# A hybrid decoder layer on one core: the steady plan of its recurrence in another order

## The chip, the cores and the metric

The kernel runs on one core of one Trainium2 chip. The metric is the time of one execution on the device, in microseconds (us). Three runs of the kernel before have a median of 2458.68 (2458.55 to 2462.13).

## The reference, cut to what matters

One layer over 2048 tokens of width 1024, batch 1. The change lies in the first sub-layer, whose input projection feeds two groups of heads: an SSD group and an RWKV7 group with a recurrence over the tokens.

```python
def _rwkv7_scan(r, w, k, v, za, zb):
    def step(S, inp):
        r_t, w_t, k_t, v_t, a_t, b_t = inp
        sa = jnp.einsum("bhij,bhj->bhi", S, a_t)
        S = S * w_t[:, :, None, :] + sa[..., None] * b_t[:, :, None, :] + v_t[..., None] * k_t[:, :, None, :]
        return S, jnp.einsum("bhij,bhj->bhi", S, r_t)
...
xn = _rms_norm(h, pre_mix_norm[l])
proj = (xn @ w_in[l]).astype(jnp.float32)
p_ssd, p_rwkv = jnp.split(proj, [SSD_COLS], axis=-1)
y_ssd = _ssd_mixer(p_ssd, ...)
y_rwkv = _rwkv7_mixer(p_rwkv, ...)
mix = jnp.concatenate([y_ssd, y_rwkv], axis=-1).astype(h.dtype) @ w_out[l]
h = h + _rms_norm(mix, post_mix_norm[l])
hn = _rms_norm(h, pre_ffn_norm[l])
u = _causal_dwconv(hn @ ffn_w_up[l], ffn_conv_w[l], ffn_conv_b[l])
gate, val = jnp.split(u, 2, axis=-1)
f = (jax.nn.silu(gate) * val) @ ffn_w_down[l]
h = h + _rms_norm(f, post_ffn_norm[l])
```

## The kernel before

The program has three stages: `phase_R` computes the input projections, the convolution of the SSD group and the RWKV7 recurrence in 16 blocks of 128 tokens (R0 to R15); `phase_S` does the SSD group, the output projection and the norms; `phase_F` the feed-forward part. The change touches only `phase_R` and its seam to `phase_S`.

The recurrence of a block is done in two chunks of 64 tokens with the usual triangular form: products of the scaled keys and receptances (gram), a triangular solve, and products with the state. A block's work is cut into some 295 small steps, each of which issues the instructions of one engine (a PE step a whole group of matmuls). A step is written `block.name.arguments/part`. What the parts are:

- `load`: /0 VectorE copies the halo of the token tile xt, /1 SP loads the rows, /2 ScalarE squares and sums them, /3 and /4 GpSimd the root (a power), /5 and /6 ScalarE scales and rounds, /7 GpSimd the low half, /8 and /9 SP transposes both halves into xt by DMA, /10 SP stores xt.
- `d.0` to `d.13`: a group of 24 matmuls each for 128 columns of the RWKV7 projection (line 737). Two neighbours (d.0 and d.1, and so on) share a PSUM bank. An even one is a TensorE step only. An odd one has /0 TensorE, /1 and /2 ScalarE (line 981), /3 and /4 VectorE (line 984), for both; after that the bank is free. d.0 and d.1 give WA and GL, d.2 to d.5 the keys tk, d.6 to d.9 tr, d.10 to d.13 the values tv.
- `conv.0` to `conv.7`: the same for the SSD columns. An odd one has /0 TensorE, /1 and /2 ScalarE, /3 to /8 the taps on VectorE (line 1030), /9 ScalarE tanh, /10 VectorE, /11 SP.
- `low.0`: /0, /1, /3, /5 ScalarE, /2, /4, /6 VectorE. `low.1`: /0 and /5 TensorE (zw, za), four ScalarE steps behind each.
- `scan` /0 GpSimd, /1 VectorE, /2 GpSimd, /3 and /4 ScalarE. `keys` /0 GpSimd, /1 ScalarE. `norm` /0 TensorE, /1 and /2 ScalarE, /3, /8, /9, /11 VectorE, the rest GpSimd. `receptance`: VectorE.
- `gram.0`, `gram.1`: /0 TensorE (line 1163), /1 and /2 VectorE masks.
- `solve`: /0 to /8 SP (the diagonal blocks out to memory and back, start values), /9 to /70 the substitution, 62 instructions on VectorE in one chain (lines 1203 and 1209, two inputs from SBUF each), /71 to /78 SP (the result out and back).
- `turn`: VectorE (line 1281), then `merge.0` and `merge.1`: /0 TensorE (lines 1297, 1301), /1 and /2 ScalarE.
- `own.c` /0 and /1 TensorE (pq, lines 1334 and 1340), /2 ScalarE; `update.c` /0 TensorE, /1 and /2 ScalarE; `state.c` /0 and /1 GpSimd, /2 TensorE (pS), /3 and /4 VectorE (S), /5 TensorE (pq), /6 and /7 ScalarE, which empty pq (line 1402).
- `values` /0 TensorE, /1 and /2 ScalarE, /3 TensorE, /4 VectorE. `transposed.c`: GpSimd for c = 0, one TensorE and one ScalarE step. `gate` /0 TensorE, /1 ScalarE.
- `finish.0`: /0 ScalarE, /1 VectorE, /2 GpSimd, /3 GpSimd (a power, line 1437), /4 GpSimd (line 1441). `finish.1`: /0 TensorE (yt), /1 to /4 ScalarE (line 1453), /5 and /6 GpSimd (lines 1463, 1464), /7 ScalarE, /8 GpSimd, /9 SP.

The order of every engine's queue is written out by hand. `HEAD` is the order of block 0 and much of block 1. `PLAN` is one round of the steady state and is walked 13 times (`it` = 2 to 14): `f` stands for block `it`, `n` for the one after it, `b` for `it` - 1 and `a` for `it` - 2, so that a round holds steps of up to four blocks, and each of a block's 295 steps comes in one of the rounds. A step that has been done already is skipped. `TAIL` creates what is left (in the order of the allocations), and `ORDER` gives the order in which that is issued. Each engine takes its steps strictly in the order of the text; waits between engines follow from the data and the buffers. PSUM is held in rings: two banks for the d and conv pairs, three for zw, za, nq, gr, bt, vt and bo, one each for pq (Q), for pu and pS (U), and for pw, po, zg, yt and one of the gr (B). The order of the text is also the order in which these rings are handed out.

```python
for it in range(2, iters - 1):
    for step in PLAN.split():
        ...
        n = it + {"n": 1, "f": 0, "b": -1, "a": -2}[who]
        if 0 <= n < iters:
            blocks[n].do(name, *(int(v) for v in a), only=int(part) if part else None)
```

## Time and profile before

| | us |
|---|---|
| median of three runs | 2458.68 |
| the profiled execution, its own time | 2461.38 |
| its span, first to last instruction | 2459.6 |
| TensorE busy | 2353.0 (96%) |
| VectorE busy | 1879.6 (76%) |
| ScalarE busy | 1200.3 (49%) |
| GpSimd busy | 1061.2 (43%) |

The profile is one execution. Its engines are PE (TensorE matmuls), PEld (weight loads), DVE (VectorE), ACT (ScalarE), POOL (GpSimd) and SP (the queue that issues DMAs). A timeline row has the start and the length in us, the engine, the line of the kernel, the operation, what it writes and reads, the shape and the number of instructions merged into the row, and in brackets the idle time of the engine just before it with the one who ended it. The steps of the recurrence fill about the first 800 us of the span, and a round of the plan is repeated there with the same pattern.

### The profile page before, as it was taken

The numbers are of one execution on the slowest core, as the hardware profiler recorded it, in microseconds if no ns is written. First come the engines' busy times: TensorE is split into PE (matmuls) and PEld (weight loads), VectorE is DVE, ScalarE is ACT, GpSimd is POOL, SyncE is SP. The second block draws the span as 40 slices with busy tenths as digits, with TensorE's granted clock in tenths as the row PEclk, the third lists the DMA queues.
The fourth block names the chain that finished last, engine by engine and source line by source line (L and its number), as shares of the span: only waits on it lengthen the run. The fifth ranks groups of instructions, "written<-read, shape, count | busy, mean of one in ns | idle before, by whom it ended". The sixth has DMA issues, their size and how long they took to land.

```text
span 2459.6 us, 53351 instructions
## 1 busy us (share of the span) xinstructions
PE 2353.0 (96%) x20986; PEld 1483.9 (60%) x20988; DVE 1879.6 (76%) x3790; ACT 1200.3 (49%) x2471; POOL 1061.2 (43%) x1134
## 2 busy tenths in 40 slices
...
DMA packets 344412, 319.11 MB, mean 130 GB/s; under 512 B 203232, under 2 KB 248672, under 8 KB 340832
## 3 DMA queue, kind: packets, MB, share of 16 engines
...
q14 instruction: 87, 0.71, 0.1%
...
## 4 chain that ended last, share of the span: by engine, by line
PE 40%; DVE 7%; issue 3%; POOL 3%; ACT 2%; DMA 2%; SPq 0%; POOLq 0%; DVEq 0%; ACTq 0%
PE u L2288 25%; PE d L2528 12%; DVE w L2141 1%; PE o L2002 1%; PE l L2653 1%; DVE C L2310 1%; DVE p L2345 1%; DVE a L2345 1%; POOL fa L2139 0%; DMA hs<-HN 0%; PE z L1787 0%; POOL m L2040 0%; DVE dw L2492 0%; DMA HN<-hT 0%; DVE b L2139 0%
## 5 line engine op out<-in xcount | busy, mean ns | idle before, releaser
L2288 PE MATMUL u<-b,w 128*128 128x512 f16 x3696 | 807.0, 380 | 16.3 <-DVE C L2310 7.9
L2288 PEld LDWEIGHTS <-w 128*128 128x128 f16 x3696 | 362.3, 98 | 456.1 <-issue 23.3
L737 PE MATMUL d<-xt,wr 128*128 128x129 f16 x5376 | 337.8, 224 | 34.4 <-DMA xt<-xh 14.6
L737 PEld LDWEIGHTS <-wr 128*128 128x128 f16 x5376 | 319.6, 100 | 42.5 <-issue 27.4
L2528 PE MATMUL d<-dw,fa 128*128 128x512 f16 x1512 | 334.6, 380 | 5.8 <-DVE acc L2541 3.7
L2528 PEld LDWEIGHTS <-fa 128*128 128x128 f16 x1596 | 156.5, 98 | 200.8 <-issue 13.6
L2310 DVE TENSOR_TENSOR C<-u,C 128x512 f32<-128x512 f32 x220 | 150.7, 686 | 157.0 <-PE u L2288 140.9
L737 PE MATMUL c<-xt,wc 128*128 128x131 f16 x3072 | 194.3, 224 | 4.9 <-ACT tv L981 2.8
L737 PEld LDWEIGHTS <-wc 128*128 128x128 f16 x3072 | 182.0, 98 | 9.3 <-issue 4.6
L2541 DVE TENSOR_TENSOR acc<-d,acc 128x512 f32<-128x512 f32 x212 | 139.5, 681 | 43.8 <-PE d L2528 39.7
L2139 POOL TENSOR_TENSOR fa<-p,fa 128x512 f16<-128x512 f32 x100 | 133.9, 1350 | 75.5 <-ACT fa L2134 75.5
L2345 DVE SCALAR_TENSOR_TENSOR p<-C,fpar,p 128x1024 f32<-128x1024 f32 x88 | 121.1, 1376 | 45.5 <-ACT p L2341 45.2
L1203 DVE TENSOR_TENSOR tmp<-atl,xl 128x60 f32<-128x60 f32 (+24 forms) x465 | 129.0, 277 | 11.7 <-DMA atl<-ATd 0.2
L2306 ACT ACTIVATE C<-u 128x512 f32<-128x512 f32 x88 | 52.2, 593 | 169.5 <-PE u L2288 134.8
L2141 DVE SCALAR_TENSOR_TENSOR w<-us,w 128x512 f16<-128x512 f32 x132 | 126.6, 969 | 9.4 <-ACT w L2134 8.7
L1030 DVE SCALAR_TENSOR_TENSOR ca<-c,cw,ca 128x128 f32<-128x128 f32 x360 | 114.4, 344 | 21.1 <-ACT ca L1020 17.2
L2345 DVE SCALAR_TENSOR_TENSOR a<-C,fpar,a 128x1024 f32<-128x1024 f32 x88 | 122.7, 1394 | 6.9 <-ACT a L2341 5.5
L2134 ACT ACTIVATE fa<-p 128x512 f16<-128x512 f32 x110 | 65.6, 622 | 114.5 <-DVE p L2358 87.4
L2134 ACT ACTIVATE w<-us 128x512 f16<-128x512 f32 x132 | 79.8, 624 | 80.2 <-PE u L2288 29.1
L1209 DVE TENSOR_TENSOR xl<-xl,tmp 128x60 f32<-128x60 f32 (+24 forms) x465 | 99.2, 213 | 13.9
L2261 POOL TENSOR_TENSOR us<-us,us 128x512 f32<-128x512 f32 x51 | 78.0, 1532 | 50.0 <-DVE w L2141 28.7
L1787 PE MATMUL z<-ws,xs 128*128 128x512 f16 x384 | 93.5, 386 | 0.1
...
## 6 DMA issues: line engine op xcount, KB each, us to landing
...
```

The source lines that it names most:

```text
L737: nc.tensor.matmul(ps, w[:, a, kt, :], xt[:, b, kt, cols], start=n == 0, stop=n == 3 * KT - 1)
L1030: V.scalar_tensor_tensor(out=acc[:, q], in0=m["rc", e][:, q, k:k + 128], scalar=cw[:, e + q, k:k + 1], in1=acc[:, q], op0=ALU.mult, op1=AL ...
L1203: chain.tensor_tensor(out=self.tmp[:, :k, :n], in0=self.atl[:, j, j + 1:32].unsqueeze(1).to_broadcast([P, k, n]), in1=self.xl[:, :k, j:j + ...
L1209: chain.tensor_tensor(out=self.xl[:, :k, j + 1:32], in0=self.xl[:, :k, j + 1:32], in1=self.tmp[:, :k, :n], op=ALU.add)
L2134: S.activation(h, src, AF.Copy, **({} if scale is None else {"scale": scale}))
L2139: {"V": V, "G": G_}[engine].tensor_tensor(out=l, in0=src, in1=h, op=ALU.subtract)
L2141: V.scalar_tensor_tensor(out=l, in0=src, scalar=scale, in1=h, op0=ALU.mult, op1=ALU.subtract)
L2288: nc.tensor.matmul(bk[at], self.w[i][:, u, k, :], self.half.b[i][:, k, v, :], start=start and n == 0, stop=n == 11, skip_group_check=True)
L2310: op("V", .61, lambda: V.tensor_tensor(out=part(j, x), in0=bk[at], in1=part(*a), op=ALU.add), (("u", 4 * s + at), (*(c0, c1)[a[0]], a[1])) ...
L2345: V.scalar_tensor_tensor(out=o[j], in0=C[j][:, 2 - d:1026 - d], scalar=cw(g, 2 - d), in1=o[j], op0=ALU.mult, op1=ALU.add)
L2528: nc.tensor.matmul(bk[s, t], pairs[m].a[i][:, u, t * P:t * P + P], pairs[m].w[n][0][:, v, :], start=new and m == 0 and u == v == 0, stop=m ...
L2541: V.tensor_tensor(out=acc[j][:, t], in0=bk[s, t], in1=acc[j][:, t], op=ALU.add)
```

## The change

`PLAN` is replaced by another order of a round of 295 steps. Some steps also change rounds: steps 27 to 34 of the solve, d.11/1, d.11/3, load/8, load/9, state.1/0, state.1/1 and gate/1 go from one round to the next one's start (from `f` to `b`, `n` to `f`, `b` to `a`), and state.1/6 from `a` to the end of `b`. In `TAIL`, R14.d.11 is put ahead of the list, and in `ORDER` the 15 steps that the 13 rounds now leave over are put in front; all else of both is as before (the lines are only wrapped anew).

```diff
@@ -294,37 +294,37 @@
 R1.conv.7/11 R1.solve/74 R1.solve/75 R1.solve/78 R1.solve/76 R2.load/10 R1.transposed.1/1 R1.solve/77
 """
 PLAN = """
-f.d.0 b.solve/35 a.state.1/6 a.state.1/7 b.solve/36 b.solve/37 a.finish.0/0 b.solve/38 f.d.1/0 b.d.13/2 b.conv.7/9
-b.d.13/1 a.finish.0/1 b.solve/39 b.solve/40 b.solve/41 b.solve/42 b.solve/43 b.solve/44 b.solve/45 b.solve/46
-a.finish.0/2 b.transposed.0/2 b.d.13/3 b.values/3 b.d.13/4 a.finish.0/3 f.d.1/1 f.d.1/2 f.d.2 b.conv.5/11 f.scan/2
-b.solve/47 a.finish.0/4 f.d.1/3 a.finish.1/0 f.low.0/0 b.values/0 b.solve/48 f.low.0/1 f.d.1/4 f.low.0/3 b.solve/49
-f.d.3/0 n.load/0 b.transposed.1/1 b.solve/50 b.solve/51 f.low.0/2 f.low.0/4 a.finish.1/1 b.solve/52 a.finish.1/4
-b.solve/53 a.finish.1/2 b.solve/54 a.state.1/3 a.finish.1/3 a.finish.1/5 b.solve/55 b.solve/56 f.low.1/0 f.d.4
-b.values/4 f.d.3/1 f.d.3/2 f.d.3/4 f.d.3/3 a.finish.1/6 a.finish.1/7 f.load/10 f.d.5/0 f.d.6 b.solve/57 b.solve/58
-f.low.1/1 f.low.1/3 a.state.1/4 f.d.5/2 b.solve/59 b.solve/60 b.solve/61 b.solve/62 b.solve/63 b.solve/64 b.solve/65
-f.low.1/5 f.d.5/1 b.values/1 f.d.5/3 f.d.5/4 f.low.1/4 f.low.1/6 f.keys/0 f.d.7/0 f.d.8 f.d.9/0 b.solve/66 f.low.1/2
-f.scan/0 b.solve/67 b.solve/68 f.low.1/9 b.values/2 f.d.7/2 b.conv.7/10 f.low.1/7 b.solve/69 b.solve/70 f.d.7/4
-f.d.7/1 f.d.7/3 f.scan/1 b.solve/73 f.keys/1 f.norm/0 f.low.1/8 f.norm/4 f.norm/5 f.norm/1 f.d.9/2 b.solve/72 f.d.9/1
-b.own.0/0 f.norm/7 b.solve/74 f.scan/3 f.norm/6 a.finish.1/8 b.solve/71 f.conv.0 f.norm/2 f.d.9/3 f.conv.1/0
-b.solve/75 f.d.9/4 f.norm/3 b.state.0/0 f.scan/4 f.norm/8 f.conv.1/1 f.conv.1/2 f.conv.1/4 b.own.0/1 f.conv.1/3
-b.own.0/2 f.conv.1/6 f.norm/10 b.solve/76 f.conv.1/5 f.conv.1/7 b.conv.7/11 f.conv.2 b.turn/0 b.solve/78 b.turn/1
-f.conv.1/8 f.norm/11 f.conv.1/9 f.conv.3/0 a.finish.1/9 b.merge.0/0 f.low.0/5 f.norm/12 b.solve/77 b.merge.0/1
-b.merge.0/2 f.conv.1/10 f.conv.4 b.merge.1/0 f.conv.3/1 f.conv.3/2 f.norm/9 f.receptance/0 n.load/1 b.merge.1/2
-f.gram.0/0 b.merge.1/1 f.gram.1/0 b.update.0/0 f.conv.3/4 f.receptance/1 b.update.0/1 b.update.0/2 f.conv.3/3
-f.conv.3/6 f.solve/8 b.low.0/6 f.conv.3/8 n.load/2 f.conv.3/5 f.gram.0/1 f.gram.0/2 f.conv.1/11 f.gram.1/2
-f.transposed.0/0 f.gram.1/1 n.load/3 f.conv.3/7 f.receptance/2 n.load/4 f.conv.5/0 b.gate/0 f.receptance/4 f.conv.3/9
-f.conv.3/10 b.state.0/2 b.state.0/1 b.state.0/5 f.conv.5/1 n.load/5 n.load/6 f.solve/1 b.state.0/4 f.solve/0
-f.conv.5/3 f.conv.5/5 n.load/7 f.conv.5/2 f.solve/2 f.receptance/3 f.conv.6 f.solve/3 f.conv.5/4 b.gate/1 f.conv.7/0
-b.state.0/3 b.state.0/6 b.state.0/7 b.own.1/0 f.conv.5/6 b.own.1/1 b.state.1/0 f.conv.3/11 f.conv.7/1 b.state.1/1
-f.transposed.0/1 f.conv.5/8 f.conv.5/7 f.conv.7/2 f.conv.5/9 f.conv.7/3 f.conv.7/5 f.conv.7/7 b.own.1/2 f.conv.7/4
-f.solve/4 f.conv.7/6 f.conv.7/8 f.solve/5 f.conv.5/10 f.solve/6 f.d.10 f.d.11/0 f.d.11/1 f.solve/7 n.load/8
-b.update.1/0 b.update.1/1 b.update.1/2 f.solve/9 f.d.11/2 f.solve/10 f.solve/11 f.solve/12 f.solve/13 f.solve/14
-f.solve/15 f.solve/16 f.solve/17 f.solve/18 f.solve/19 f.solve/20 f.solve/21 f.solve/22 f.d.11/3 f.solve/23 f.solve/24
-f.solve/25 f.solve/26 f.solve/27 f.solve/28 f.solve/29 f.solve/30 f.solve/31 f.solve/32 f.solve/33 f.solve/34 n.load/9
-f.transposed.1/0 f.d.12 f.d.11/4 b.state.1/5 b.state.1/2 f.d.13/0
+b.d.11/1 a.state.1/0 a.state.1/7 a.finish.0/0 b.d.11/3 b.solve/27 b.solve/28 b.transposed.0/2 f.load/8 a.state.1/1
+b.d.13/2 b.d.13/1 b.solve/29 a.finish.0/1 b.solve/30 b.solve/31 b.transposed.1/1 b.d.13/3 b.solve/32 b.solve/33
+b.d.13/4 a.gate/1 f.load/9 f.d.0 f.d.1/0 f.d.1/1 f.d.2 a.finish.0/2 a.finish.0/3 b.solve/34 b.solve/35 b.conv.5/11
+b.values/0 b.solve/36 b.solve/37 f.d.1/3 f.d.1/2 f.d.1/4 b.solve/38 b.solve/39 f.d.4 f.low.0/0 f.low.0/1 f.low.0/3
+f.low.0/2 f.low.1/0 b.conv.7/9 a.finish.0/4 a.finish.1/0 a.finish.1/1 b.solve/40 b.solve/41 b.solve/42 b.solve/43
+b.solve/44 b.solve/45 b.solve/46 b.solve/47 a.finish.1/4 b.solve/48 f.d.3/0 f.low.0/4 b.solve/49 b.solve/50 b.solve/51
+b.values/1 a.finish.1/3 a.finish.1/2 b.values/2 f.low.1/1 b.solve/52 b.solve/53 b.solve/54 b.solve/55 b.solve/56
+b.solve/57 b.solve/58 a.finish.1/5 b.values/3 b.solve/59 a.state.1/4 f.d.3/1 f.d.3/3 f.d.5/0 f.d.3/2 f.d.5/1 f.d.5/2
+f.d.3/4 b.own.0/0 f.low.1/5 f.low.1/6 f.d.5/3 b.solve/60 a.finish.1/6 f.d.6 b.solve/61 b.solve/62 f.low.1/9 f.d.5/4
+b.solve/63 b.solve/64 f.low.1/4 b.solve/65 f.low.1/3 a.finish.1/7 f.d.7/0 f.keys/0 f.keys/1 f.low.1/7 b.solve/66
+b.solve/67 b.solve/68 f.d.8 f.low.1/2 b.solve/69 b.solve/70 b.solve/73 b.solve/71 b.solve/74 f.scan/0 f.norm/0
+a.finish.1/8 f.d.7/1 a.state.1/3 f.d.7/3 f.d.7/2 b.solve/72 f.low.1/8 f.d.7/4 f.d.9/0 b.conv.7/10 f.scan/2 n.load/0
+f.norm/1 f.conv.0 f.conv.1/0 f.scan/1 a.finish.1/9 b.values/4 f.norm/2 f.norm/3 b.conv.7/11 f.d.9/1 f.d.9/2 f.norm/4
+f.scan/3 f.d.9/3 f.d.9/4 f.norm/6 f.norm/5 n.load/1 b.own.0/1 b.solve/75 f.conv.1/1 f.scan/4 f.norm/9 f.norm/7
+f.conv.1/2 b.own.0/2 f.norm/8 f.conv.1/3 f.conv.2 f.conv.3/0 f.conv.1/4 f.conv.1/5 f.conv.1/6 b.solve/76 b.turn/0
+b.turn/1 f.conv.3/1 f.conv.1/7 f.conv.1/8 f.conv.3/3 f.norm/10 b.solve/78 f.conv.3/2 f.norm/11 f.norm/12 b.merge.0/0
+b.merge.0/2 f.receptance/0 f.conv.4 f.conv.1/9 b.solve/77 f.solve/8 b.merge.0/1 b.merge.1/0 n.load/2 f.gram.0/0
+f.conv.3/4 f.conv.3/5 f.conv.3/6 b.merge.1/1 f.receptance/4 f.conv.1/10 b.merge.1/2 n.load/3 f.conv.1/11 n.load/4
+f.gram.1/0 b.update.0/0 b.update.0/2 b.state.0/0 f.conv.3/7 f.gram.0/1 f.gram.0/2 f.gram.1/2 f.gram.1/1 f.conv.3/8
+f.receptance/2 b.state.0/1 b.update.0/1 f.conv.5/0 f.load/10 f.solve/1 b.state.0/2 f.conv.3/9 f.solve/0 f.conv.3/10
+f.receptance/3 b.state.0/5 b.state.0/6 f.solve/3 f.solve/2 b.state.0/4 f.conv.5/1 f.transposed.0/0 f.conv.6
+f.conv.3/11 f.conv.7/0 f.conv.5/3 f.solve/4 f.low.0/5 b.low.0/6 f.receptance/1 f.conv.5/5 b.state.0/3 f.conv.5/2
+f.conv.5/7 b.state.0/7 f.conv.5/4 f.conv.5/6 b.own.1/0 b.own.1/1 n.load/5 n.load/6 f.conv.7/1 f.conv.7/2 f.conv.5/8
+n.load/7 b.own.1/2 f.conv.7/3 f.d.10 f.conv.7/5 f.conv.5/9 f.d.11/0 f.conv.7/4 f.conv.7/6 b.update.1/0 f.d.11/2
+f.transposed.0/1 f.transposed.1/0 b.update.1/1 f.conv.7/7 f.solve/7 f.conv.7/8 f.solve/5 b.update.1/2 b.state.1/5
+b.state.1/2 f.conv.5/10 f.solve/6 f.d.12 f.d.13/0 f.d.11/4 b.gate/0 f.solve/9 f.solve/10 f.solve/11 f.solve/12
+f.solve/13 f.solve/14 f.solve/15 f.solve/16 f.solve/17 f.solve/18 f.solve/19 f.solve/20 f.solve/21 f.solve/22
+f.solve/23 f.solve/24 f.solve/25 f.solve/26 b.state.1/6
 """
 TAIL = """
-R14.solve R13.state.1 R13.finish.0 R14.d.13 R14.conv.7 R14.transposed.0 R13.values R14.conv.5 R15.load
+R14.d.11 R14.solve R13.state.1 R13.finish.0 R14.d.13 R14.conv.7 R14.transposed.0 R13.values R14.conv.5 R15.load
 R14.transposed.1 R13.own.0 R13.state.0 R13.turn R13.merge.0 R13.merge.1 R13.update.0 R14.low.0 R13.gate R13.own.1
 R13.update.1 R15.d.0 R15.d.1 R15.d.2 R15.d.3 R15.d.4 R15.low.0 R15.low.1 R15.d.5 R13.finish.1 R15.scan R14.values
 R15.keys R15.d.6 R15.norm R15.d.7 R15.d.8 R15.d.9 R15.receptance R15.d.10 R14.turn R14.merge.0 R15.d.11 R14.own.0
...
-R14.conv.7/9 R13.state.1/6 R13.state.1/7 R14.conv.7/10 R13.state.1/3 R14.conv.7/11 R14.solve/35 R15.d.0/0
+R14.d.11/1 R13.state.1/0 R14.d.11/3 R14.solve/27 R14.solve/28 R15.load/8 R13.state.1/1 R14.solve/29 R14.solve/30
+R14.solve/31 R14.solve/32 R14.solve/33 R13.gate/1 R15.load/9 R14.solve/34 R14.conv.7/9 R13.state.1/6 R13.state.1/7
...
```

256 lines of the change are left out of this document (128 added, 128 removed).

## The prediction

> **What bounds the kernel now.** I read the span first, then the busy time by windows over the recurrence, then TensorE's timeline through one block, and last VectorE, ScalarE and GpSimd where they end a wait of TensorE.
>
> ```profile
> span 2459.6 us, 53351 instructions
> ...
> core 0: us, PE busy (x) PEld busy (x) DVE busy (x) ACT busy (x) POOL busy (x), PEclk, DMA share, GB/s
> 159.47:751.77 592.30, 579.21 (x10014) 545.01 (x10009) 478.04 (x1561) 379.12 (x888) 254.92 (x276) 1.00 0.32 72
> ```
>
> The window runs from the gram products of block 2 to those of block 14, so 12 rounds of the plan: 592.30 / 12 = 49.36 us a round. TensorE is busy for 579.21 of it, VectorE for 478.04, at a granted clock of 1.00. The order is therefore worth at most what TensorE idles in a round. One round of its timeline (start, length, and in brackets the idle time and who ended it) shows where:
>
> ```profile
> 215.00 2.97 PE L737 MATMUL c<-xt,wc 128*128 128x131 f16 x48
> 218.38 0.68 PE L1334 MATMUL pq<-UV,G 64*64 64x64 f32 x16 [0.41 <-ACT ysb L1402]
> 219.00 1.16 PE L1340 MATMUL pq<-S,AR 128*128 128x128 f32 x8
> 219.99 0.60 PE L1243 MATMUL bt<-cst,BK 128*128 128x128 f32 x4
> 220.43 2.92 PE L737 MATMUL d<-xt,wr 128*128 128x129 f16 x48
> ...
> 226.94 1.55 PE L737 MATMUL d<-xt,wr 128*128 128x129 f16 x24
> 228.87 2.93 PE L737 MATMUL d<-xt,wr 128*128 128x129 f16 x48 [0.37 <-DVE tv L984]
> 231.63 1.50 PE L1270 MATMUL bo<-tr,cst 128*128 128x128 f32 x12
> 233.00 1.54 PE L737 MATMUL d<-xt,wr 128*128 128x129 f16 x24
> 234.37 0.61 PE L1449 MATMUL yt<-cst,ysb 128*128 128x128 f32 x4
> 234.91 1.09 PE L1258 MATMUL vt<-cmat,tv 128*64 128x128 f32 x16
> 235.94 1.55 PE L737 MATMUL d<-xt,wr 128*128 128x129 f16 x24
> 237.32 0.39 PE L1071 MATMUL zw<-WX,wl 128*128 128x128 f16 x4
> ...
> 237.77 4.30 PE L737 MATMUL d<-xt,wr 128*128 128x129 f16 x72
> 241.91 0.39 PE L1071 MATMUL za<-WX,wl 128*128 128x128 f16 x4
> ...
> 251.92 2.96 PE L737 MATMUL c<-xt,wc 128*128 128x131 f16 x48
> ...
> 255.43 0.69 PE L1297 MATMUL pw<-XW,G 32*32 32x32 f32 x30 [0.22 <-DVE XW L1281]
> 256.05 1.57 PE L737 MATMUL c<-xt,wc 128*128 128x131 f16 x24
> 257.55 0.69 PE L1301 MATMUL po<-XT,XW 32*32 32x32 f32 x32
> ```
>
> Groups overlap, so I cost a group by the distance from its start to the next start. A d group costs 1.38 undisturbed (237.77 to 241.91 is three). A c group costs 1.50 when small f32 tiles follow (256.05 to 257.55), and a c group ahead of another 1.40 (2.97 - 1.57). The three bracketed waits are then:
> - d.0 behind d.13: 228.87 - 226.94 = 1.93, less 1.38: 0.55. It needs the PSUM bank that d.11/4 reads last, and that step stands on VectorE behind 26 steps of the solve.
> - own.1/0 behind conv.6 and conv.7: 218.38 - 215.00 = 3.38, less 2.90: 0.48. It needs its bank emptied by state.0/6 and /7.
> - merge.0 behind conv.2 and conv.3: 255.43 - 251.92 = 3.51, less 2.90 and 0.04 for its first two products: 0.57. It needs the turned block, which stands on VectorE behind five conv taps.
>
> Together 1.60 us a round, 49.36 - 1.60 = 47.76 without them. The new order cannot give more than 12 x 1.60 = 19 us here.
>
> **The change, part by part.** No instruction is added, removed or altered. Every step keeps its duration and only its place in its queue changes, so the cost of each edit is a wait gone or a wait come. Steps left unfinished by the last round are done in the first lines of the closing order, as much work as before.
>
> *The three old waits.* The other rows that I use are these, first of ScalarE, then of VectorE, GpSimd:
>
> ```profile
> 212.25 1.04 ACT L926 ACTIVATE xh<-xin 128x1024 bf16<-128x1024 f32 x1
> ...
> 217.57 0.76 ACT L1402 ACTIVATE ysb<-pq 64x256 f32<-64x256 f32 x2
> ...
> 223.39 0.37 ACT L981 ACTIVATE tv<-d,omu 128x128 f32<-128x128 f32 x1 [2.60 <-PE d L737]
> ...
> 235.65 1.51 ACT L1453 ACTIVATE yln<-yt,par 128x128 f32<-128x128 f32 x4
> ...
> 241.43 0.59 ACT L1263 ACTIVATE UV<-vt 64x512 f32<-64x512 f32 x1
> ```
>
> ```profile
> 221.60 0.18 DVE L1203 TENSOR_TENSOR tmp<-atl,xl 128x31 f32<-128x31 f32 x1
> ...
> 225.21 0.35 DVE L984 SCALAR_TENSOR_TENSOR tv<-d,mus,tv 128x128 f32<-128x128 f32 x1 [0.38 <-ACT tv L981]
> ...
> 231.04 0.24 DVE L1209 TENSOR_TENSOR xl<-xl,tmp 128x75 f32<-128x75 f32 x1
> ...
> 232.77 0.96 DVE L1203 TENSOR_TENSOR tmp<-atl,xl 128x60 f32<-128x60 f32 x1
> ...
> 237.02 0.68 DVE L1275 TENSOR_TENSOR tv<-bo,tv 128x512 f32<-128x512 f32 x1
> ...
> 238.72 1.20 DVE L1203 TENSOR_TENSOR tmp<-atl,xl 128x49 f32<-128x49 f32 x1
> ...
> 240.19 0.42 DVE L1391 TENSOR_TENSOR S<-tS,pS 64x256 f32<-64x256 f32 x1
> 240.65 0.20 DVE L1203 TENSOR_TENSOR tmp<-atl,xl 128x42 f32<-128x42 f32 x1
> ```
>
> ```profile
> 230.88 1.65 POOL L1437 TENSOR_TENSOR gnr<-gnv,mhalf 128x8 f32<-128x8 f32 x1
> ...
> 232.61 1.04 POOL L1441 TENSOR_TENSOR ysb<-ysb,gnr 128x512 f32<-128x512 f32 x1
> 237.24 1.27 POOL L1463 TENSOR_TENSOR yln<-yln,tv 128x512 f32<-128x512 f32 x1 [3.58 <-ACT yln L1453]
> 238.59 1.27 POOL L1464 TENSOR_TENSOR yln<-yln,tg 128x512 f32<-128x512 f32 x1
> ```
>
> own.1/0: before, n.load/5 and /6 stand ahead of state.0/6 on ScalarE. Now state.0/6 and /7 go ahead of them, with only conv.5/1, low.0/5 and conv.5/2 between, and conv.6 and conv.7 (2.90) cover these. I take the 0.48 as gone. What that cover hides would cost the same 0.48 if it were lost. n.load/5 and /6 go back by these steps, and with them, behind GpSimd's n.load/7, the transposes f.load/8 and /9 on SP, which d.0 needs:
>
> ```profile
> 219.23 1.30 SPq L941 DMA_TRANSPOSE xt<-xin  x1
> ```
>
> Before, the last was issued by 220.53, 8.3 ahead of d.0 (228.87). I count some 2 less in the new order; 6 us should still do, as nothing in the profile shows d.0 waiting for them.
>
> d.0: d.11/4 now stands ahead of the solve, and d.11/3 behind 18 of its steps. With D and the steps' pace as worked out below, they are over by D + 7.1 (2.3, 18 steps at 0.25, 0.35), and d.0 comes at D + 7.9. I take the 0.55 as gone.
>
> merge.0: the turn now stands ahead of the last two taps of conv.1, and the solve that feeds it ends about as early as before relative to merge.0. I estimate that the turn ends some tenths before TensorE is there, from the two taps that it now precedes; I take the 0.57 as gone and keep it as the upper end.
>
> *New waits on ScalarE.* n.load/2 (1.04) now stands between merge.0/1 and merge.1/1. Whoever follows it waits: merge.1/1 and /2 release the bank for gram.1/0, and before they were done just in time. The bound is 0 to 1.04; since most of it runs beside merge.1 and gram.0, I take 0.1. update.1/1 and /2 have only the two transpose groups as cover, which comes out even: 0.05. A d group ahead of own.0's small tiles costs 0.1 more, as conv does (1.50 against 1.40). Sum of the new: 0.25, or 0 to 1.8 by the bounds, merge.0 included.
>
> *The solve on VectorE, the tightest place.* Let D be the start of d.11, 220.43 + 1.38 = 221.81. In the new order TensorE has from D to d.6: d.11, update, one transpose group, d.12 and two state products as before (226.94 - 221.81 = 5.13), another transpose group 0.44, d.13 1.38, gate 0.99 (as the pq of eight), d.0 to d.2 4.14, values/0 1.03, d.4 1.38, low.1/0 0.45: finish.1/0 starts at D + 14.9. Then 0.54, d.3 1.38, values/3 1.37, d.5 1.48, own.0/0 0.62, low.1/5 0.45: d.6 at D + 20.8. d.6 needs the bank that d.3/4 reads, and d.3/4 stands on VectorE behind the solve up to step 59.
>
> That stretch of the solve, steps 9 to 59, takes 240.65 - 221.60 = 19.05 in the profile. Out of it go the wait of 0.38, the two steps held for 0.96 and 1.20 instead of 0.23 (1.70 in all), values/4 and d.3 with their wait (238.72 - 237.02, 1.6), two short steps that move (0.35), and state.1/4 (0.45): 14.6 is left. It starts when ScalarE has d.11 (223.39 is D + 1.58), plus 0.37 and one step of VectorE: D + 2.3. A wait of 0.9 for d.1/1 comes in, since d.1 ends only at D + 10.9. So step 59 comes at D + 17.8. state.1/4, d.3/3 and d.3/4 take 1.1 more: D + 18.9, nearly 2 us ahead of d.6, if nothing holds VectorE.
>
> Something can: both held steps stand exactly beside a GpSimd instruction (232.77 in 232.61's, 238.72 in 238.59's), and end 0.1 after it. The Trainium skill, SBUF — State Buffer, Who interferes with whom, says that a VectorE instruction with two SBUF inputs and a GpSimd one that reads SBUF exclude each other for the whole instruction, whichever started first. These rows agree. The power of 1.65 at 230.88 does not: the solve's step at 231.04 ran through it in 0.24. By the rule that power would hold a step too, and the time would be that of the first rival; by the trace it is mine.
>
> GpSimd's finish.1/5 starts when ScalarE has its four parts: D + 14.9, plus 0.61, 1.51 and some 0.5 for values/1 between them: D + 17.6, with step 59 at 17.8. So I count one step held to the end of finish.1/5, D + 18.9, and d.3/4 at D + 20.1: 0.7 before d.6. Nothing waits.
>
> Sum: 49.36 - 1.60 + 0.25 = 48.0 us a round, 1.35 less. Over 12 rounds 16.2; for the seams at both ends I count nothing, within one round's 1.4 either way. The profiled execution reads 2461.4, 1.8 us more than its span, and would become 2445.2; the median 2458.7, from which I predict, becomes 2442.5. Behind the recurrence the same queues follow in the same order, so the whole saving is kept.
>
> **Rivals.**
>
> *Two steps held.* If VectorE comes to finish.1/5 0.25 late, step 58 is held by it and step 59 by finish.1/6, which follows at once: d.3/4 at D + 21.4, d.6 waits 0.6 to 0.7. A round is 48.65: 12 x 0.7 = 8.4 us, 2450 to 2451. For it: the two starts are 0.2 apart. Against: the held steps of the profile were single ones.
>
> *The order only moves its waits.* VectorE is busy 478.04 of 592.30, and the margins above are tenths; if they are lost elsewhere (merge.0, d.0) to the sum of 1.3, the round stays near 49.3: 2454 to 2463.
>
> *Slower: the solve closes a longer loop.* d.11 releases the solve, the solve d.3/4, that d.6, and d.6 after 28.6 us of TensorE the next d.11. Behind its margin of 0.7, every microsecond on VectorE counts fully. If each of four GpSimd instructions holds a step, the power (1.65) and finish.0/4 (1.04) as well as finish.1/5 and finish.1/6 (1.27 each), 1.65 + 1.04 + 1.27 less three steps of 0.23 come on top of my sum, 3.3; the wait for d.1 hides 0 to 0.9 of it, the margin 0.7. d.6 waits 1.7 to 2.6, a round is 49.7 to 50.6, and the time 2463 to 2474. It beats the old order from a wait of 1.35 on. For it: more of the solve now lies beside these four. Against: the step that ran through the power, and that VectorE reaches finish.0/4 while it waits for d.1.
>
> **How the numbers follow.** About 0.2% (4.9 us) can be told from no change. My forecast has a chance of 0.50, with a range of its own of 2438 to 2447; two steps held 0.21; moved waits 0.14; slower 0.15. The first two are faster by more than 0.2%: 0.71; the third is the same: 0.14; the fourth slower: 0.15. The range of 8 in 10 takes the first two and most of the third: 2437 (every wait gone and both seams gaining) to 2459.
>
> **What would show it.** Right: gram to gram 47.8 to 48.2 us in the new timeline, no bracket at d.0 behind tv or at pq behind ysb, at most one solve step held between d.1/4 and d.3/4, and TensorE's busy time unchanged. The first rival shows a bracket of some 0.6 at the fourth d pair, released by tk, and two held steps in a row. The last shows that bracket at 1.7 or more, and gram to gram at 49.7 or more. A bracket at pw or at gr above 0.3 would prove my step on the turn or on n.load/2 wrong; a round under 47.7 my floor.

## The result and the profile after

| | before | after |
|---|---|---|
| median (four runs each), us | 2458.61 | 2483.03 |
| ratio, 95% interval | | 1.010 (1.0083 to 1.0117) |
| the profiled execution, us | 2461.38 | 2488.25 |
| gram to gram, mean of 12 rounds, us | 49.36 | 51.01 |

The change makes the kernel slower by 1%, where 0.7% faster was forecast. A second set of four runs of the changed kernel gave 2482.23, a ratio of 1.0082 (1.0067 to 1.0097). The page and its busy time by windows, gram of block 2 to gram of block 14:

```profile
span 2486.5 us, 53299 instructions
```

```profile
core 0: us, PE busy (x) PEld busy (x) DVE busy (x) ACT busy (x) POOL busy (x), PEclk, DMA share, GB/s
158.46:770.62 612.16, 585.34 (x10014) 549.66 (x10009) 497.84 (x1560) 381.85 (x889) 261.42 (x276) 1.00 0.30 68
```

612.16 / 12 = 51.01 us a round, at a granted clock of 1.00 as before, with the same instructions. (One round, the one of 52.30 that starts at 310.90, had a mean granted clock of 0.98; the profile of the second set has no such round, and its mean is 50.89.) So 19.9 us of the 26.9 between the two spans lie in these rounds: 12 x (51.01 - 49.36). The first rounds take 1.0 less, and the close, from gram of block 14 to the first feed-forward product, 449.7 instead of 442.7. VectorE's busy time has grown by 19.8, though it does the same work: some of its instructions last longer. One round of the timeline, all engines (start, length, in brackets the idle time and who ended it):

```profile
260.25 2.49 PE L1164 MATMUL gr<-AR,BK 64*128 64x128 f32 x32
...
268.77 0.68 PE L1335 MATMUL pq<-UV,G 64*64 64x64 f32 x16
...
270.38 2.92 PE L738 MATMUL d<-xt,wr 128*128 128x129 f16 x48
...
279.67 4.30 PE L738 MATMUL d<-xt,wr 128*128 128x129 f16 x72
...
283.42 0.37 ACT L982 ACTIVATE GL<-d,omu 128x128 f32<-128x128 f32 x1 [0.42 <-DVE WA L985]
...
283.82 0.35 DVE L985 SCALAR_TENSOR_TENSOR GL<-d,mus,GL 128x128 f32<-128x128 f32 x1 [0.44 <-ACT GL L982]
...
289.46 1.27 POOL L1464 TENSOR_TENSOR yln<-yln,tv 128x512 f32<-128x512 f32 x1 [6.04 <-ACT yln L1454]
289.62 1.17 DVE L1204 TENSOR_TENSOR tmp<-atl,xl 128x49 f32<-128x49 f32 x1
...
290.81 1.26 POOL L1465 TENSOR_TENSOR yln<-yln,tg 128x512 f32<-128x512 f32 x1
290.83 1.31 DVE L1210 TENSOR_TENSOR xl<-xl,tmp 128x49 f32<-128x49 f32 x1
...
292.25 0.39 PE L1076 MATMUL za<-WX,wl 128*128 128x128 f16 x4
...
293.25 0.89 ACT L982 ACTIVATE tk<-d,omu 128x128 f32<-128x128 f32 x3 [2.60 <-DVE tk L985]
...
293.65 0.35 DVE L985 SCALAR_TENSOR_TENSOR tk<-d,mus,tk 128x128 f32<-128x128 f32 x1 [0.43 <-ACT tk L982]
...
294.06 4.32 PE L738 MATMUL d<-xt,wr 128*128 128x129 f16 x72 [1.42 <-DVE tk L985]
...
307.81 0.69 PE L1298 MATMUL pw<-XW,G 32*32 32x32 f32 x30 [0.22 <-DVE XW L1282]
...
310.28 0.69 PE L1302 MATMUL po<-XT,XW 32*32 32x32 f32 x32 [0.28 <-ACT XW L1309]
```

Two of the old waits are gone as forecast: pq at own.1 (268.77) and the group with d.0 (279.67) have no bracket. New ones have come. The largest is d.6's, 1.42 behind tk. From the last za product to d.6 it is 294.06 - 292.25 = 1.81 here, and 0.22 where nothing waits, so 1.59. Ahead of it stand two things that the prediction did not have in its sum: two steps of the solve in a row held to the end of a GpSimd instruction (1.17 and 1.31 instead of 0.21), and ScalarE's d.3/2 idle for 2.60 until VectorE has done d.3/3, after which VectorE waits 0.43 for it. The same pair of waits stands at d.1 (0.42 and 0.44).

Taken this way over the 12 rounds, as the distance between two starts on TensorE less the same distance where nothing waits, a round of 51.01 holds 1.58 at d.6, 0.81 at merge.0, 0.35 at merge.1 and 0.41 at gram.1. What is left is 47.86; the prediction had a floor of 47.76.

What merge.0 waits for can be followed on SP, whose queue changed too. In the new order finish.1/9 (YR), conv.7/11 (XC) and n.load/1 (xin, 512 KB of rows) stand ahead of solve/75 to /78, which fetch the solve's result back from memory (XT). Before, the first half of XT stood ahead of all three, and the rows behind all of it. The kernel before, then the changed one:

```profile
298.61 0.82 SPq L1221 DMA_DIRECT2D XT<-XTd  x2
...
301.84 1.36 SPq L754 DMA_DIRECT2D xin<-in_x_dram  x1
```

```profile
301.86 0.57 SPq L755 DMA_DIRECT2D xin<-in_x_dram  x1
302.61 1.84 SPq L1222 DMA_DIRECT2D XT<-XTd  x4
...
306.85 0.90 DVE L1282 STREAM_TRANSPOSE XW<-XT 32x256 f32<-32x256 f32 x2 [0.37 <-DMA XT<-XTd]
```

The last row is the turn. It waits for XT in nine of the twelve rounds, 0.32 to 1.50 us; in the kernel before it never waits.

### The profile page after: what moved, and what is told of

Its sections match the earlier page's. It is cut to its first block, busy times and chain, and to the rows that moved or that the text cites. A ratio compares the mean times of both kernels' runs of the same rounds, so it can differ in the third digit from the quotient of the medians.

```text
span 2486.5 us, 53299 instructions
## 1 busy us (share of the span) xinstructions
PE 2360.4 (95%) x20988; PEld 1488.6 (60%) x20988; DVE 1896.3 (76%) x3790; ACT 1203.9 (48%) x2471; POOL 1066.9 (43%) x1134
## 4 chain that ended last, share of the span: by engine, by line
PE 41%; DVE 6%; issue 2%; POOL 2%; ACT 2%; DMA 2%; SPq 0%; DVEq 0%; POOLq 0%; ACTq 0%
PE u L2289 26%; PE d L2529 12%; DVE w L2142 1%; PE o L2003 1%; PE l L2654 1%; DVE C L2311 1%; DVE p L2346 1%; DVE a L2346 1%; DMA hs<-HN 1%; POOL fa L2140 0%; PE z L1788 0%; DVE dw L2493 0%; DMA HN<-hT 0%; ACT hl L2022 0%; POOL m L2041 0%
## 5 line engine op out<-in xcount | busy, mean ns | idle before, releaser
L738 PE MATMUL d<-xt,wr 128*128 128x129 f16 x5376 | 336.1, 223 | 48.7 <-DVE tk L985 17.1
L1210 DVE TENSOR_TENSOR xl<-xl,tmp 128x60 f32<-128x60 f32 (+24 forms) x465 | 122.7, 264 | 13.1
L1204 DVE TENSOR_TENSOR tmp<-atl,xl 128x60 f32<-128x60 f32 (+24 forms) x465 | 112.5, 242 | 14.4 <-DMA atl<-ATd 0.4
```

Of the source, the lines that this page charges most:

```text
L738: nc.tensor.matmul(ps, w[:, a, kt, :], xt[:, b, kt, cols], start=n == 0, stop=n == 3 * KT - 1)
L1204: chain.tensor_tensor(out=self.tmp[:, :k, :n], in0=self.atl[:, j, j + 1:32].unsqueeze(1).to_broadcast([P, k, n]), in1=self.xl[:, :k, j:j + ...
L1210: chain.tensor_tensor(out=self.xl[:, :k, j + 1:32], in0=self.xl[:, :k, j + 1:32], in1=self.tmp[:, :k, :n], op=ALU.add)
```

## The experiments

The runs take the causes one by one: the order in which two engines read one bank, the steps that a GpSimd instruction holds, n.load/2, the old waits in the kernel before, and the places of GpSimd's and SP's work. All runs stand in this table: the mean round and TensorE's mean wait in it at d.6 and at the two merges, each from one profile, and the ratio to the kernel before, measured beside it. e1 to e3, e5, e8 to e10, e12 to e14, e16 and e17 start from the changed kernel, e4, e6, e7, e11 and e18 from the kernel before.

| run | round, us | d.6 | merge.0 and .1 | ratio (95%) |
|---|---|---|---|---|
| before | 49.36 | 0 | 0.61 | |
| after | 51.01 | 1.58 | 1.16 | 1.0100 (1.0083 to 1.0117) |
| e15 after again | 50.89 | 1.58 | 1.11 | 1.0082 (1.0067 to 1.0097) |
| e1 ScalarE's reads first | 49.57 | 0.89 | 0.73 | 1.0008 (0.9998 to 1.0017) |
| e5 the same, d pairs alone | 50.12 | 0.88 | 1.00 | 1.0034 (1.0023 to 1.0045) |
| e2 fills for finish.1/5, /6 | 48.93 | 0 | 0.89 | 1.0001 (0.9991 to 1.0012) |
| e12 both | 48.60 | 0 | 0.65 | 0.9959 (0.9946 to 0.9972) |
| e3 n.load/2 later | 51.40 | 1.59 | 1.08 | 1.0122 (1.0105 to 1.0139) |
| e9 e1 and SP's order | 49.46 | 0.88 | 0.66 | 1.0016 (1.0004 to 1.0029) |
| e8 finish moved, together | 49.40 | 0 | 0.11 | 1.0015 (1.0006 to 1.0024) |
| e10 finish elsewhere | 49.97 | 0 | 1.34 | 1.0049 (1.0031 to 1.0068) |
| e13 finish in two places | 48.82 | 0 | 0.10 | 0.9978 (0.9969 to 0.9988) |
| e14 finish in three places | 48.39 | 0 | 0.12 | 0.9956 (0.9940 to 0.9972) |
| e16 and rows later on SP | 48.47 | 0 | 0.12 | 0.9955 (0.9938 to 0.9972) |
| e17 and n.load/2 later | 48.85 | 0 | 0.15 | 0.9978 (0.9968 to 0.9988) |
| e4 before, d.11/4 early | 49.47 | 0 | 0.61 | 0.9998 (0.9988 to 1.0008) |
| e6 before, n.load/5 to /7 later | 51.10 | 0 | 0.43 | 1.0105 (1.0090 to 1.0120) |
| e7 before, d.11 and d.13 early | 49.46 | 0 | 0.61 | 1.0002 (0.9990 to 1.0013) |
| e11 before, ScalarE's reads first | 49.93 | 0 | 0.26 | 1.0039 (1.0026 to 1.0053) |
| e18 e7 and d.7's order | 48.59 | 0 | 0.44 | 0.9959 (0.9944 to 0.9973) |

Three of these means hold rounds at a lower granted clock. In e5 it is the last two (51.26 at 0.98, 51.48 at 0.95; the other ten have a mean of 49.87), in e6 three rounds (52.1 at 0.97; the other nine have 50.77), in e10 seven (0.98; the other five have 49.56).

**The order of two readers (e1, e5).** The theory to test: two engines that read one PSUM bank are kept in the order of the text. The steps are moved in the text alone, past steps of other engines, so that every queue stays as it was. The edit is shown for d.3; the same was done for d.1, d.7, conv.3 and conv.5.

```diff
 f.d.3/1
+f.d.3/2
 f.d.3/3
 f.d.5/0
-f.d.3/2
 f.d.5/1
```

> The changed kernel with only the text order of one bank's readers altered: of d.1, d.3, d.7, conv.3 and conv.5 both ScalarE reads (and low.0/5 with conv.5/2) stand ahead of VectorE's first read in the text. Every engine's own queue is as it was. Theory A (readers of one PSUM bank on two engines are kept in the order of the text, so that ScalarE's second read waits for VectorE's first and VectorE's second for that): the 2.60 of ScalarE at L982 behind tk, the 0.42 at GL, and VectorE's 0.44 and 0.43 behind them are gone; the solve comes 0.4 earlier to finish.1/5, so that one step is held instead of two; d.6's wait of about 1.6 is gone; a round goes from 51.01 to 49.2 to 49.6, the time to 2459 to 2467. Theory B (the wait of d.6 is GpSimd's alone, which holds two steps of the solve; the order of the readers costs only what VectorE shows at once): VectorE's two brackets go, both steps stay held, d.6 waits 0.7 to 1.2, a round is 50.1 to 50.6, the time 2472 to 2478. Theory C (the text order sets nothing between engines): nothing changes, 51.0 and 2483.

The timeline of e1, the stretch before d.6:

```profile
237.68 1.17 DVE L1210 TENSOR_TENSOR xl<-xl,tmp 128x49 f32<-128x49 f32 x1
...
238.34 0.62 ACT L982 ACTIVATE tk<-d,omu 128x128 f32<-128x128 f32 x2
...
238.88 1.31 DVE L1204 TENSOR_TENSOR tmp<-atl,xl 128x42 f32<-128x42 f32 x1
...
240.66 0.87 DVE L985 SCALAR_TENSOR_TENSOR tk<-d,mus,tk 128x128 f32<-128x128 f32 x3
...
241.41 4.30 PE L738 MATMUL d<-xt,wr 128*128 128x129 f16 x72 [0.73 <-DVE tk L985]
```

ScalarE now reads d.2 and d.3 in one go (238.34, two instructions, no idle time), long ahead of VectorE, whose three evictions run without a gap. 1.44 of the 1.65 us that the change had cost a round are gone, with the same queues: theory A holds for the readers, theory C is out. But both steps of the solve are still held, and d.6 still waits 0.89: theory B holds for the rest of d.6's wait. VectorE is one step further when finish.1/5 starts, and so the held steps are the next ones: 49 and 42 columns, where they were 49 and 49.

> The changed kernel with ScalarE's reads ahead of VectorE's in the text for d.1, d.3 and d.7 alone; conv.3 and conv.5 stay as in the changed kernel. The run with all five showed 49.57 a round. If the price of the text order lies in the solve's chain (d.1 and d.3): d.6's bracket goes from 1.42 to 0.73 as there, merge.1's 0.28 behind ScalarE's XW stays, a round is 50.2 to 50.4, the time 2469 to 2473. If it lies in conv.3 and conv.5: d.6's bracket stays near 1.4 and a round at 50.9 or more.

With d.1, d.3 and d.7 alone d.6's wait is 0.88 as in e1, and the 0.39 at merge.1 behind XW stays (0.02 in e1). That is the first line of the expectation. How the 1.44 divides is told best by the rounds at full clock, 50.90 in the changed kernel, 49.87 in e5 and 49.57 in e1: about 1.0 for the d pairs and 0.3 for the conv pairs.

The Trainium skill, PSUM — Partial Sum Buffer, section PSUM bank collisions raise a hardware error, says that the scheduler of the compiler's back end adds a dependency between any two instructions on different engines that touch the same bank and quadrant, "reads and writes alike". The waits in these traces are what such a rule would make of the text's order. That this rule makes them is not shown here; a kernel in which the two read in either order was not tried.

**The held steps (e2, e12).** GpSimd's two instructions beside the solve are replaced by fills, which read nothing.

```diff
-lambda: G_.tensor_tensor(out=self.yln, in0=self.yln, in1=self.tv, op=ALU.add),
-lambda: G_.tensor_tensor(out=self.yln, in0=self.yln, in1=self.tg, op=ALU.mult),
+lambda: G_.memset(self.yln, 0.5),
+lambda: G_.memset(self.yln, 0.25),
```

> The changed kernel with finish.1/5 and /6 on GpSimd replaced by fills of yln with a constant, which read nothing (the bonus term and the gate are left out). Theory B (GpSimd's reads hold two steps of the solve): both held steps (1.17 and 1.31) become 0.22, d.3/4 comes some 2.0 earlier, d.6's wait of about 1.6 is gone, though ScalarE's wait behind tk stays; a round is 49.3 to 49.7, the time 2460 to 2467. Theory A by itself (the order of the readers costs the time, the held steps are covered): the held steps go, but d.6 keeps a wait of 0.4 or more, and a round is 50.2 or more.

```profile
286.86 0.53 POOL L1464 MEMSET yln<- 128x512 f32 x1 [6.00 <-ACT yln L1454]
287.03 0.21 DVE L1204 TENSOR_TENSOR tmp<-atl,xl 128x49 f32<-128x49 f32 x1
287.28 0.21 DVE L1210 TENSOR_TENSOR xl<-xl,tmp 128x49 f32<-128x49 f32 x1
...
289.67 0.39 PE L1076 MATMUL za<-WX,wl 128*128 128x128 f16 x4
...
289.89 4.30 PE L738 MATMUL d<-xt,wr 128*128 128x129 f16 x72
```

The same steps of the solve take 0.21, though both start inside a fill (286.86 to 287.39), and d.6 comes 0.22 after the last za product: no wait. This is theory B again. (The fills are also shorter, 0.53 for 1.27; in e8, e13 and e14 below the two instructions are whole and stand elsewhere, and d.6 waits for nothing there either.) The Trainium skill, SBUF — State Buffer, section Who interferes with whom, states that a VectorE instruction with two SBUF inputs contends with a GpSimd instruction that reads SBUF and not with one that only writes it; both runs agree. The round, 48.93, is shorter than either line expected. Its twelve rounds are 5.1 us shorter than those of the kernel before, and yet the time is the same, 1.0001, as the close took 447.3 instead of 442.7.

> The changed kernel with both causes out at once: the text order of the five pairs, and finish.1/5 and /6 as fills that read nothing (bonus and gate left out). Alone the first gave a round of 49.57, the second 48.93, against 51.01. If the two are separate and make up the whole loss at d.6 and merge.1: no bracket at d.6 or po, a round of 48.1 to 48.5, the time 2452 to 2456 with the longer close. If they are one loss seen twice: 48.7 to 48.9, as with the fills alone.

48.60, a little over the first range, with nothing left at d.6 and 0.02 at merge.1. The two causes are separate, but at d.6 they overlap: taking out the order gives 0.69 of its 1.58, taking out the held steps all of it. What is left of the loss is 0.63 at merge.0 and 0.31 at gram.1.

**n.load/2 (e3).** My term for it was 0.1.

```diff
-n.load/2
 f.gram.0/0
...
 b.merge.1/2
+n.load/2
```

> The changed kernel with n.load/2 on ScalarE moved behind merge.1/1 and /2. My prediction's term for this edit was 0.1, with 0 to 1.04. If the wait ahead of gram.1 is n.load/2's: gram.0 with gram.1 goes from 2.49 to 2.08 in the timeline, and a round is shorter by 0.3 to 0.4, 3.6 to 5 us in all (2478 to 2480). If the seam of the loop d.11, solve, d.3/4, d.6 sets the round: gram.1's wait goes, but d.6 waits as much longer, and a round stays within 0.1 of 51.0.

```profile
320.03 1.91 POOL L1239 TENSOR_TENSOR BK<-BK,Pi 128x1024 f32<-128x1024 f32 x1
320.31 1.92 DVE L1042 SCALAR_TENSOR_TENSOR ca<-ct,ca 128x256 f32<-128x256 f32 x1 [0.20 <-ACT ct L1037]
...
324.02 0.46 ACT L1021 ACTIVATE ca<-c,cb,cw 128x128 f32<-128x128 f32 x1 [1.94 <-DVE ca L1031]
...
324.93 0.68 PE L1335 MATMUL pq<-UV,G 64*64 64x64 f32 x16 [0.92 <-ACT ysb L1403]
```

gram.1's wait is gone, so it was n.load/2's (0.41, between the bounds 0 and 1.04), and yet a round is 0.39 longer (0.51 against the 50.89 of the second set), which neither line of the expectation had. The rows show both mechanisms at work in a chain: GpSimd comes later with n.load/3 and /4 and so with its product BK; conv.3/10, two inputs from SBUF, is now held past BK's end (1.92 instead of 0.41); VectorE's conv.5/3 behind it is late; ScalarE's conv.5/2 waits 1.94 for that reader (0.88 in the changed kernel); state.0/7 stands behind it; and own.1 waits 0.92.

**The old waits one at a time, in the kernel before (e4, e6, e7, e11, e18).** My sum took the three old waits as gone one by one.

```diff
 f.d.11/3
+f.d.11/4
 f.solve/23
...
 f.d.12
-f.d.11/4
```

> The kernel before with one step moved: d.11/4 on VectorE stands right behind d.11/3, ahead of the solve's steps 23 to 34. My prediction's term: d.0's wait of 0.55 for that bank is gone and nothing takes its place: a round of 48.8, 6.6 us less, 2452. Rival (VectorE's solve closes the loop already in the kernel before): the steps behind come 0.35 later, no gain or 0.1 to 0.35 lost at d.6 or merge.0, a round of 49.2 to 49.7.

```profile
231.16 1.54 PE L737 MATMUL d<-xt,wr 128*128 128x129 f16 x24 [0.54 <-DVE tv L984]
```

d.0 no longer waits, and d.2 waits 0.54 for the next bank of the ring, which d.13/4 frees behind the same solve. The wait had only moved.

```diff
 a.finish.0/1
+b.d.13/3
+b.d.13/4
 b.solve/39
...
-b.d.13/3
 b.values/3
-b.d.13/4
...
 f.d.11/3
+f.d.11/4
 f.solve/23
...
 f.d.12
-f.d.11/4
```

> The kernel before with d.11/4 right behind d.11/3 as in the run before, and d.13/3 and /4 moved ahead as well, from behind step 46 of the solve to ahead of step 39. With d.11/4 alone the wait of 0.55 moved from d.0 to d.2 (0.54, behind d.13/4) and a round was 49.47. If that is one wait that goes to whichever step of the ring is late next: the bracket at d.2 is gone, 0 to 0.3 comes at d.6 behind tk or at merge.0, a round is 48.9 to 49.2, 2453 to 2457. If VectorE's chain as a whole sets the round: the whole 0.5 comes back at d.6, a round is 49.4 to 49.5.

```profile
293.41 0.34 DVE L984 SCALAR_TENSOR_TENSOR tr<-d,mus,tr 128x128 f32<-128x128 f32 x1
...
293.79 0.37 ACT L981 ACTIVATE tr<-d,omu 128x128 f32<-128x128 f32 x1 [1.03 <-DVE tr L984]
294.05 0.62 ACT L1108 ACTIVATE sq<-kkn 128x512 f32<-128x512 f32 x1
...
294.72 1.12 PE L1117 MATMUL nq<-sq,cst 128*128 128x512 f32 x2 [0.46 <-ACT sq L1108]
```

It moved again, to norm/0 (0.46): the second expectation, at a place that it did not name. The rows show how: ScalarE's d.7/1 waits 1.03 for VectorE's d.7/4, which the text names first, and sq stands behind it on ScalarE. With d.7/1 ahead of d.7/4 in the text and nothing else changed:

```diff
 b.conv.7/10
 f.low.1/7
...
+f.d.7/1
 f.d.7/4
-f.d.7/1
```

> The kernel before with d.11/4, d.13/3 and d.13/4 early, as in the run where the wait had moved from d.0 by d.2 to norm/0 (0.46, behind ScalarE's sq, which stands behind d.7/1, which waits 1.03 for VectorE's d.7/4 of the same bank), and d.7/1 put ahead of d.7/4 in the text; the queues stay. If the readers' order carries the wait to norm/0 here: ScalarE's 1.03 and VectorE's 0.43 at tr go, nq's 0.46 goes, a round is 48.7 to 49.1 instead of 49.46, 0.3 to 0.4% faster than the kernel before. If the wait is VectorE's lateness whatever the order: it comes back at nq or merge.0, 49.3 to 49.5, no change.

```profile
290.12 0.37 ACT L981 ACTIVATE tr<-d,omu 128x128 f32<-128x128 f32 x1
...
291.59 1.08 PE L1117 MATMUL nq<-sq,cst 128*128 128x512 f32 x2
```

ScalarE reads tr's bank without a wait (290.12), nq waits for nothing, and merge.0's wait falls from 0.61 to 0.26 as well. Most rounds are 48.40, below the 48.7 to 49.1 of the first line; two of the twelve are longer, as merge.1 waits 0.81 and 1.25 for XT there (mean 48.59). The time is 0.9959 (0.9944 to 0.9973) of the kernel before: four steps moved give what 295 in a new order did not. d.7's order without the early evictions was not run alone, so how the gain divides between them is not shown. The other direction of the same rule shows in e11, where d.7/1 and conv.5/2 come first in the text:

```diff
+f.d.7/1
 f.d.7/4
-f.d.7/1
...
-f.conv.5/3
-f.conv.5/5
 f.conv.5/2
+f.conv.5/3
+f.conv.5/5
```

> The kernel before with only the text order altered where it has VectorE's reads ahead of ScalarE's second: d.7/1 ahead of d.7/4, and conv.5/3 and /5 behind conv.5/2; the queues are as they were. If the readers' order costs the kernel before too: ScalarE's waits at tr (0.86 behind L984) and VectorE's 0.43 behind it go, the norms and the turn come 0.4 earlier, merge.0's wait shrinks, a round is 48.8 to 49.1, the time 2452 to 2456. If these waits are covered in the kernel before: 49.3 to 49.4, no change of time.

```profile
264.79 1.06 ACT L946 ACTIVATE xh<-xin 128x1024 f16<-128x1024 f32 x1
...
265.76 0.44 ACT L1020 ACTIVATE ca<-c,cb,cw 128x128 f32<-128x128 f32 x1
...
266.23 0.74 DVE L1030 SCALAR_TENSOR_TENSOR ca<-c,cw,ca 128x128 f32<-128x128 f32 x2 [1.50 <-ACT ca L1020]
...
268.90 1.16 PE L1340 MATMUL pq<-S,AR 128*128 128x128 f32 x8 [0.83 <-DVE S L1391]
```

Slower by 0.57 a round, against both expectations. merge.0's wait fell from 0.61 to 0.26, but now VectorE's conv.5/3 waits 1.50 for ScalarE's conv.5/2, which stands behind n.load/5 and /6 (the row at 264.79 is /6), and own.1/1 waits 0.83 for S behind it. So neither engine is the better first reader: whoever is ready first must stand first.

The wait at own.1 was tried with n.load/5 and /6 moved back:

```diff
-n.load/5
-n.load/6
...
 b.state.0/7
+n.load/5
+n.load/6
```

> The kernel before with n.load/5 and /6 on ScalarE moved behind state.0/6 and /7, and n.load/7 on GpSimd behind state.1/1. My prediction's term: own.1's wait of 0.48 is gone and nothing takes its place: a round of 48.88, 2453. Rival (from conv.7's taps to d.13/4 VectorE is the path, so that TensorE only comes earlier to d.0 or d.2): the 0.41 at pq goes, the bracket at d behind tv grows by as much, a round is 49.2 to 49.4, 2457 to 2460.

```profile
319.49 1.06 ACT L946 ACTIVATE xh<-xin 128x1024 f16<-128x1024 f32 x1
...
320.57 0.81 ACT L1020 ACTIVATE ca<-c,cb,cw 128x128 f32<-128x128 f32 x2
...
321.41 2.15 DVE L1030 SCALAR_TENSOR_TENSOR ca<-c,cw,ca 128x128 f32<-128x128 f32 x6 [2.65 <-ACT ca L1020]
...
330.61 2.94 PE L737 MATMUL d<-xt,wr 128*128 128x129 f16 x48 [2.17 <-DVE tv L984]
```

Neither expectation held: a round is 1.41 longer where the granted clock is 1.00 (50.77). In the kernel before, the 2.2 us of the two loads fill the time in which ScalarE's conv.5/2 must wait for VectorE's conv.5/3, the reader named first. Moved behind, they leave ScalarE idle there (2.50 behind ca) and delay conv.7/1 and /2; VectorE waits 2.65 for these, its taps of conv.7 stand ahead of the solve, and d.0 waits 2.17.

**Can GpSimd's reads be put where they hold nobody (e8, e10, e13, e14, e9, e16, e17)?** All start from e1's order. In e8 finish.1/5 and /6 go behind norm/12 (with /7 to /9 behind them), and on SP conv.7/11 and n.load/1 behind solve/76:

```diff
 f.norm/12
+a.finish.1/5
+a.finish.1/6
```

> The changed kernel with three edits: the text order of the run with all five pairs; finish.1/5 and /6 on GpSimd moved from beside the solve to behind norm/12, beside the taps of conv.1 (with ScalarE's finish.1/7, GpSimd's /8 and the store /9 behind them); and on SP conv.7/11 and n.load/1 moved behind solve/75 and /76, so that the solve's result comes back ahead of the 512 KB of the next rows. If the held steps, the order of the readers and the order of the queue are the causes: no step of the solve is held, no bracket at d.6, none above 0.3 at pw, a round of 48.0 to 48.5, the time 2446 to 2452. If the queue is not what makes merge.0 wait: every other round still shows 0.7 to 1.3 at pw and the mean is 48.7 to 49.2, 2455 to 2460.

```profile
305.53 1.79 POOL L1465 TENSOR_TENSOR yln<-yln,tg 128x512 f32<-128x512 f32 x1
...
306.11 1.76 DVE L1151 TENSOR_TENSOR AR<-tr,Pi 128x512 f32<-128x512 f32 x1
...
308.02 2.06 PE L1164 MATMUL gr<-AR,BK 64*128 64x128 f32 x32 [0.82 <-POOL pnv L931]
```

No step of the solve is held by the two, d.6 and merge.0 wait for nothing, but AR is held (1.76 instead of 0.68 in e14), and gram.0, which reads AR, waits 0.82. So a round is 49.40 where 48.0 to 48.5 was expected. (The bracket names GpSimd's pnv, whose result gram does not read; AR ends at 307.87.) The price was paid at another place.

> The changed kernel with the text order of all five pairs (the first of these runs, rounds alternating between 48.9 and 50.2) and on SP finish.1/9, conv.7/11 and n.load/1 moved behind solve/75 and /76; finish.1/5 and /6 stay beside the solve. If the queue makes merge.0 wait in every other round (XT's way back from memory stands behind a store and 512 KB of rows): no bracket above 0.3 at pw, all rounds 48.8 to 49.0, the time 2450 to 2454. If merge.0 waits because the solve ends late: the bracket at pw stays, the rounds still alternate, the mean stays at 49.4 to 49.7 and the time at 2459 to 2464.

e9, the queue's edit alone on top of e1, takes merge.0's wait away in all twelve rounds (0.71 to 0.01), but merge.1 then waits 0.65, up to 1.64, and the mean stays. The turn no longer waits for XT in any round, so the queue's order was what merge.0 waited for. At merge.1 the brackets name XT's second half in three rounds (0.47 to 1.57), which e9 leaves behind the rows, and ScalarE in six (0.18 to 1.26); why ScalarE is late there was not settled. With the solve early (e14 and e16, below) merge.1 waits 0.11 and 0.12, whether the rows stand between the two parts of the solve's result or behind both.

> The changed kernel with all causes found so far taken out together: the text order of the five pairs; finish.1/5 and /6 on GpSimd behind norm/7, where VectorE waits for ScalarE, with /7 behind own.0/2 and /8 behind norm/12; solve/76 and the turn two taps of conv.1 earlier, with conv.7/11, n.load/1 and finish.1/9 on SP behind them; n.load/2 behind merge.1/2 and n.load/3, /4 behind transposed.0/0. If the held steps, the readers' order, the queue and n.load/2 are the whole of the loss: no bracket at d.6, gr or pw above 0.3, a round of 47.9 to 48.4, the time 2443 to 2450. If each wait that goes only uncovers the next: brackets of 0.3 to 1 at other places (own.1, gram.0), a round of 48.7 to 49.3, 2451 to 2460.

In e10 /5 and /6 stand behind norm/7, beside VectorE's kkn, AR and tk: these last 1.73, 1.24 and 1.76 (tk beside GpSimd's next one, sq), the turn comes late, and merge.0 waits 1.31. A round of 49.97 lies above both lines. In e13 and e14 they are taken apart and put beside VectorE's taps, which read PSUM. These are the places in e14; in e13 finish.1/8 stands behind transposed.0/0 instead:

```diff
 f.norm/12
+a.finish.1/5
...
 n.load/4
+a.finish.1/6
...
 b.update.1/0
+a.finish.1/8
```

> The changed kernel with the five pairs' text order, conv.7/11 and n.load/1 on SP behind solve/75 and /76, and GpSimd's finish work put where VectorE reads PSUM: finish.1/5 behind norm/12, /6 behind n.load/4, /7 on ScalarE behind update.0/1, /8 behind transposed.0/0. Against the run with /5 and /6 together behind norm/12 (49.40, where they held AR for 1.76 and gram.0 waited 0.82). If the place beside AR alone was the cost: gram.0's bracket is gone, gram.1 shows its 0.4 again, a round of 48.3 to 48.8, the time 2449 to 2456. If VectorE pays about 2 us a round wherever the two stand: own.1 or the solve's start waits instead, 49.1 to 49.5, 2459 to 2464.

> As the run before, with finish.1/8 behind n.load/7 on GpSimd, beside the taps of conv.7, instead of behind transposed.0/0. By the first theory 48.1 to 48.6 and 2447 to 2454, as own.1 is not held up by /8; by the second (VectorE pays wherever) 49.1 to 49.5.

```profile
299.61 1.27 POOL L1464 TENSOR_TENSOR yln<-yln,tv 128x512 f32<-128x512 f32 x1
...
301.54 0.68 DVE L1151 TENSOR_TENSOR AR<-tr,Pi 128x512 f32<-128x512 f32 x1
...
302.56 2.49 PE L1164 MATMUL gr<-AR,BK 64*128 64x128 f32 x32
```

48.82 and 48.39: the first theory. In e13 finish.1/8 still holds VectorE's receptance (1.24 instead of 0.35), and own.1/1 waits 0.34; in e14 it does not. e14 is faster than the kernel before, 0.9956 (0.9940 to 0.9972), and five of its rounds are 48.13, where 48.0 was forecast for the change as it was.

> The run with the finish work in three places (a round of 48.39, some rounds at 48.13), with conv.7/11 and n.load/1 on SP behind solve/78 and /77 too, so that both parts of the solve's result come back ahead of the 512 KB of rows. With the rows between the parts merge.0 no longer waited but merge.1/0 did, up to 1.6 in the run with the queue alone. If it is the part that stands behind the rows that comes late: po never waits, a round is 48.1 to 48.3, 2446 to 2453. If the rows then come too late for n.load/2 on ScalarE: po or gram.1 waits 0.3 to 1 for it, 48.5 to 49.

> As the run before, with n.load/2 on ScalarE behind merge.1/1 and /2. In the changed kernel that edit alone cost 0.39 a round: gram.1's 0.41 went, but transposed.0/0 on GpSimd came later, held conv.3/10 on VectorE, and by the readers' order of conv.5 state.0/7 and own.1 (0.91). With conv.5's reads in the other order that second half is gone: gram.1's 0.41 goes, own.1 waits 0 to 0.3, a round is 47.8 to 48.0. If own.1 waits as before: 48.5 to 48.8.

e16 is e14 over again (48.47, 0.9955), and its longer rounds have their wait elsewhere: in the round of 49.08 the d group waits 0.79 for the transposes of xt. In e14 it is 0.81 in the round of 49.10. That is the wait of d.0 for f.load/8 and /9, which my prediction named and took as covered; in the changed kernel itself it was covered. In e17 gram.1's wait is gone, and own.1/1 waits 0.68, as GpSimd's BK, later again, holds VectorE for 2.00. So n.load/2's 0.41 was not to be had by this move either, though the readers no longer passed it on.

> The changed kernel unaltered, to see how much of its loss lies outside the rounds. In its first profile 12 rounds were 19.9 us longer, and from the last of them to the start of the feed-forward stage it took 449.7 against 442.7. If the close of the recurrence is the rest: again 446 or more from there, the time 2481 to 2486. If that was the one execution: 441 to 445 and a profile some 5 us shorter.

The round is 50.89, and the close takes 446.6. It is longer than the 442.7 of before in every run but e1 (440.7), by 0.2 to 7.0, in those of the old order too; how much of it belongs to the change was not settled.

## Why the prediction was wrong, point by point

Added up, the floor and the 0.15 booked for update.1 and own.0 make 47.91 (47.86 measured). On top come 1.58 at d.6, where nothing was booked, 0.81 at merge.0, booked as gone, 0.41 at gram.1, booked as 0.1, and 0.35 at merge.1, which the sum did not have: 51.01.

*Floor.* Right: 47.76 worked out, 47.86 left when the new waits are taken off.

*own.1 and d.0.* Right for the changed kernel, no bracket at either. But the step behind it does not hold in general: the sum takes 1.60 off for three waits, as if a wait that goes were time won. In the kernel before d.0's wait went to d.2 and then to norm/0 as VectorE's evictions were put early (e4, e7), and the round became shorter only with the readers' order of d.7 changed too (e18). Such waits are won only if nothing behind them is late next.

*merge.0.* This step failed. I took 0.57 as gone because the turn was moved ahead of two taps; it waits 0.81, above my upper end of 0.57. In the three rounds in which the turn does not wait for XT, 0.18 to 0.19 is left at merge.0; in the nine others it waits for it, as SP in the new order fetches XT behind two stores and 512 KB of rows. With SP's order put right on top of e1's (e9), merge.0 waits 0.01, where e1 has 0.71. The prediction follows SP's queue for f.load/8 and /9 alone.

*n.load/2.* Mechanism right, size wrong: 0.41 for 0.1, within its bounds.

*merge.1.* Missing: 0.35, of which e1 takes 0.33; in e5, where conv.3's and conv.5's readers stand as in the changed kernel, it is all there (0.39).

*The solve.* The step that failed most, 1.58 of the 3.0 us that a round is longer than forecast: "So I count one step held to the end of finish.1/5, D + 18.9, and d.3/4 at D + 20.1: 0.7 before d.6. Nothing waits." D is 270.38 + 1.38 = 271.76, finish.1/5 starts at D + 17.7 (17.6 worked out), and d.3/4 ends at 294.00, D + 22.2. The 2.1 that are missing: the second held step 1.1 (1.31 - 0.21), the readers' order at tk 0.43, and the solve reaches finish.1/5 about 0.6 later than counted, 0.44 of it behind GL. So the rival "two steps held" was true, and with the readers' order taken out its price is nearly right: 0.6 to 0.7 worked out for d.6, 0.89 measured in e1. It had 0.21, and it would still have been no slower than before. (A slip in the working, 238.72 - 237.02 taken as 1.6 and not 1.70, shifts step 59 by 0.1 only.)

*The slower rival.* It named the right place (d.6 behind d.3/4) and nearly the right size (1.7 to 2.6; 1.58 measured), but its cause was not there: the power again held nobody (in e8 it runs from 279.49 to 281.14, and the steps beside it take 0.23), and VectorE was idle beside finish.0/4. The time came out above its range of 2463 to 2474, since 1.57 at merge.0, merge.1 and gram.1 and 4 to 7 us at the close come on top, which no case of mine had. (Its sentence that it beats the old order from a wait of 1.35 on says the reverse of what is meant: from there on the old order is faster.)

*What was not in it at all.* That the text's order of the readers of a bank is a wait between engines. It could have been read in the profile of before, where ScalarE waits 0.86 for VectorE's reader of tr's bank:

```profile
245.56 0.37 ACT L981 ACTIVATE tr<-d,omu 128x128 f32<-128x128 f32 x1 [0.86 <-DVE tr L984]
```

And the change interleaves the readers in d.1, d.3 and conv.3, where they had stood in order. I compared each queue with itself, and an order that lies between two queues does not show there.
